# Placing matmul operands and split-weight buffers at fixed residues modulo 256 in a two-block float32 transformer kernel

## The chip, the cores and the metric

The kernel runs on one core of one Trainium2 chip, as one program launched once. The metric is the device time of an execution in microseconds (us). Five engines work side by side: TensorE (PE in the profile; its weight loads are shown apart as PEld), VectorE (DVE), ScalarE (ACT), GpSimd (POOL) and SyncE (SP), which here only issues DMAs.

## The reference, cut to what matters

Two model blocks follow each other on 256 tokens of width 2048, all in float32. The first has two layers (modulated norm, input projection to 8192 columns, gated convolution and two-way retention, output projection; layer 0 also carries 256 context tokens). The second has one layer (input projection, two attention branches, output projection, a gated feed-forward of width 5632, and a gated last projection). What takes the time are products with large weights:

```python
u = hx @ w_in                                     # first block, 2048 x 8192, two layers
x = x + gate[:, None] * (jnp.concatenate([y_conv, y_ret], axis=-1) @ w_out)
...
proj = h @ w_in[i]                                # second block, 2048 x 6144
x = x + rms_norm(o @ w_out[i], ln_mix_post[i])
g, u = jnp.split(h @ w_gate_up[i], 2, axis=-1)    # 2048 x 11264
f = (jax.nn.silu(g) * u) @ w_down[i]              # 5632 x 2048
gate = jax.nn.sigmoid(rms_norm(x, ln_pli[i]) @ w_pli_gate[i])
```

## The kernel before

**Split products.** Each weight tile (two slices of 128 rows by up to 512 columns) arrives by a DMA of SyncE's queue in a `raw` buffer (four of them). `split` then writes its rounded part `whi` on ScalarE (line 277) and the rest `wlo` on VectorE (line 278), each in one of three rotating buffers of 4096 bytes a partition. The activations are split in the same way (high part `xh`, low part `xl`, next to each other in one buffer). A product of weight and activation is the sum of hi by hi, hi by lo and lo by hi, all accumulated in PSUM; they are issued by `Block.steps` at line 332. A matmul has a stationary operand of 128 columns, which is loaded first (PEld), and a moving operand that streams past it. In the profile's rows the moving operand's tile is named behind PEld's: `mm<-a,whi` has moving `a` and stationary `whi`.

**Three forms of the product.** In mode "fm" the weights are stationary: with 512 tokens (layer 0, and k of layer 1) three products of 512 columns for each 128 by 128 weight; with 256 tokens ("wide") one product of 512 columns, whose moving operand is xh and xl one behind the other, and one of 256 columns (`wlo` with xh). In mode "tm" the activation is stationary and 512 columns of `whi` or `wlo` move. `a0` to `a15` hold the activations of the first block (high and low part 2048 bytes apart), `h0` to `h15`, `o0` to `o15` and `f0` to `f43` those of the second (1024 bytes apart).

**Order.** TensorE's order is that of the code (a manual schedule); what runs beside it (retention heads, attention heads, the modulation vectors of the next layer) is pumped in between the products. The other engines are ordered by the framework's scheduler. The start of the kernel (`mod0_cols`, lines 454 to 471) multiplies the conditioning vectors by `w_mod`, with a stationary operand of only 4 columns, woven with the first products of the layer.

**Where buffers lie.** The framework's pools place buffers one behind the other from low addresses; only the pool `ap` of `a0` to `a15` is filled from the top. An operand's address in its partition, modulo 256, follows from the sizes of all that lies below it. Buffers of 512 bytes or its multiples keep the residue from one 128-column slice to the next, so each group of products has one pair of residues throughout. The table in the section on the change has them.

**Decay masks.** `retention` builds four 128 by 128 masks for each head on ScalarE (lines 535 to 538) from the constant tile `cr`; `layer_tables` makes the decay rates `lg` and the vectors `dec` on VectorE (lines 516 and 522).

Of the kernel before, what the change touches and what calls it, by code (L numbers as in the profile page):

```python
# [14 lines left out]
ALU = mybir.AluOpType  # L15
# [12 lines left out]
PRI = 400  # L28
HOT = 1000
HS = 128.0 ** -0.5  # L30


CA = {}
# [4 lines left out]
def _layout(d, spec):  # L38
    o = 0
    for n, w in spec:  # L40
# [3 lines left out]


NCA = _layout(CA, [("ident", 128), ("ones", 128), ("comb", 2), ("nhalf", 8)])
NCR = _layout(CR, [("ropec", 256), ("ropes", 256), ("dabs", 128), ("dof", 128), ("dob", 128),
                   ("pos", 8)])
NCB = _layout(CB, [("negtri", 128), ("negones", 128), ("md", 128), ("cmul", 384),
                   ("onehot", 384), ("negm", 384)])  # L50

# [9 lines left out]
def constants():  # L61
    f = np.float32
    ca = np.zeros((P, NCA), f)
    ca[:, slice(*CA["ident"])] = np.eye(P, dtype=f)
    ca[:, slice(*CA["ones"])] = 1.0
    o = CA["comb"][0]
    ca[0, o] = ca[2, o] = ca[1, o + 1] = ca[3, o + 1] = 1.0
    ca[:, slice(*CA["nhalf"])] = -0.5

    cr = np.zeros((P, NCR), f)  # L70
    p = np.arange(P)
    t = np.arange(L)
    inv = f(10000.0) ** (-np.arange(32, dtype=f) / f(32))
    pos = np.where((p // 64)[:, None] == 0, (t // 64)[None], (t % 64)[None]).astype(f)
    ang = (pos * inv[p % 32][:, None]).astype(f)
    cr[:, slice(*CR["ropec"])] = np.cos(ang)
    sign = np.where(p % 64 < 32, -1.0, 1.0).astype(f)
    cr[:, slice(*CR["ropes"])] = np.sin(ang) * sign[:, None]
    j = p[:, None]
    i = p[None, :]  # L80
    cr[:, slice(*CR["dabs"])] = np.abs(i - j)
    cr[:, slice(*CR["dof"])] = 128 + i - j
    cr[:, slice(*CR["dob"])] = 128 + j - i
    o = CR["pos"][0]
    for a in range(2):
        tt = p + 128 * a
        cr[:, o + a] = tt + 1
        cr[:, o + 2 + a] = L - tt
        cr[:, o + 4 + a] = L - 1 - tt
        cr[:, o + 6 + a] = tt  # L90

    cb = np.zeros((P, NCB), f)
    cb[:, slice(*CB["negtri"])] = -(j > i).astype(f)
    cb[:, slice(*CB["negones"])] = -1.0
    cb[:, slice(*CB["md"])] = (j < i)
    d = 128 + p[:, None] - np.arange(256)[None]
    mult = (d >= 0) * ((d <= 128) * 1.0 + (d % 4 == 0) + (d % 16 == 0))
    o = CB["cmul"][0]
    cb[:, o:o + 256] = mult
    cb[:, o + 256:o + 384] = mult[:, 128:]  # L100
    x = np.arange(384)
    dd = 255 - x
    dc = np.maximum(dd, 1).astype(f)
    large = 16 + (np.log(dc / f(16)) / f(math.log(128.0)) * f(16)).astype(np.int32)
    large = np.minimum(large, 31)
    bucket = np.where(dd < 16, np.maximum(dd, 0), large)
    cb[:32, slice(*CB["onehot"])] = np.arange(32)[:, None] == bucket[None]
    bad = ~((dd >= 0) & ((dd <= 128) | (dd % 4 == 0)))
    cb[:, slice(*CB["negm"])] = np.where(bad, f(NEG), f(0))[None]
    return ca, cr, cb  # L110
# [3 lines left out]
def kernel(ctx: ExitStack, tc: tile.TileContext, x, c, cx, c_ctx, norm_w, w_mod, b_mod,  # L114
# [14 lines left out]

    consts = ctx.enter_context(tc.tile_pool(name="consts", bufs=1))  # L130
    wraw = ctx.enter_context(tc.tile_pool(name="wraw", bufs=4))
    wsp = ctx.enter_context(tc.tile_pool(name="wsp", bufs=3))
    rp = ctx.enter_context(tc.tile_pool(name="rp", bufs=1))
    sm = ctx.enter_context(tc.tile_pool(name="sm", bufs=2))
    tb = ctx.enter_context(tc.tile_pool(name="tb", bufs=3))
# [35 lines left out]
    vr_ = {}  # L171

    def load_vec(g):
        vr = mk(at, [P, 512], "sc")[:, :P] if g == 2 else mk(sm, [P, P], "vr", bufs=1)
        n0 = 0
        for n, cnt in VEC_ROWS[g]:
            nc.sync.dma_start(out=vr[n0:n0 + cnt, :], in_=srcs[n])
            V[n] = vecs[:, g * P + n0:g * P + n0 + cnt]
            n0 += cnt
        vr_[g] = vr, n0  # L180
# [87 lines left out]
    pri = [0]  # L268
    turn = [0]

    def split(raw, nk, width=512, parts=None):
        if parts is None:
            parts = (mk(wsp, [P, 2, 512], "whi", F32R)[:, :nk, :width],
                     mk(wsp, [P, 2, 512], "wlo", F32R)[:, :nk, :width])
        hi, lo = parts
        with tc.high_priority(offset=pri[0]):
            nc.scalar.copy(out=hi, in_=raw)  # L277
            nc.vector.tensor_tensor(out=lo, in0=raw, in1=hi, op=ALU.subtract)  # L278
        return hi, lo

    class Block:
# [17 lines left out]
        def load(self, kk, col, parts):  # L299
            c0, wd = col  # L300
            raw = mk(wraw, [P, 2, 512], "raw")[:, :len(kk), :wd]
            nc.sync.dma_start(out=raw, in_=self.w[kk[0] * P:(kk[0] + len(kk)) * P, c0:c0 + wd]
                              .rearrange("(k p) n -> p k n", p=P))
            return split(raw, len(kk), wd, parts)

        def steps(self, kk, parts=None):

# [46 lines left out]
    p1 = ExitStack()  # L354
    ap_ = p1.enter_context(tc.tile_pool(name="ap", bufs=1, side="right", reuse_waits="tile"))
    big = p1.enter_context(tc.tile_pool(name="big", bufs=1))
    t1 = p1.enter_context(tc.tile_pool(name="t1", bufs=1))
    st0 = ExitStack()
    wst = st0.enter_context(tc.tile_pool(name="wst", bufs=3))
# [17 lines left out]
    def R_(name):  # L377
        a, b = CR[name]
        return cr[:, a:b]
# [3 lines left out]
    load_x(0)  # L383
    load_x(1)
    turn_vec(0)
    s2 = mk(consts, [P, KT, 2], "s2")
    nc.scalar.activation(out=s2[:, :, 0], in_=V["c"], func=AF.Silu)
    nc.scalar.activation(out=s2[:, :, 1], in_=V["cctx"], func=AF.Silu)
    s4 = mk(t1, [P, KT, 4], "s4", F32R)
# [27 lines left out]
        rin[s] = rsq(mean_eps(ss[:, 0], 2, D), 2, f"rq{s}")  # L417


    modc = [[mk(consts, [P, 48], f"mod{l}{v}") for v in range(2)] for l in range(2)]  # L420

    def mod_bg(todo):

# [85 lines left out]
    def layer_tables(l):  # L509

        lg = []
        for d, src in enumerate((ret_decay_f, ret_decay_b)):
            e = mk(t1, [P, 8], f"lg{d}")
            nc.sync.dma_start(out=e, in_=src[l].partition_broadcast(P))
            nc.scalar.activation(out=e, in_=e, func=AF.Exp)
            nc.vector.tensor_scalar(out=e, in0=e, scalar1=-1.0, scalar2=None, op0=ALU.mult)
            lg.append(e)
        dec = mk(t1, [P, 4, 2, 8], "dec")
        o = CR["pos"][0]
        for q in range(4):  # L520
            for a in range(2):
                nc.vector.tensor_scalar(out=dec[:, q, a, :], in0=lg[q % 2],
                                        scalar1=cr[:, o + 2 * q + a:o + 2 * q + a + 1], scalar2=None,
                                        op0=ALU.mult)
        nc.scalar.activation(out=dec, in_=dec, func=AF.Exp)
        lgt["lg"], lgt["dec"] = lg, dec

    def retention(l, h, qT, kT, v, streams, Y):
# [5 lines left out]
        eb = dm[:, 3, :]  # L534
        nc.scalar.activation(out=dm[:, 0, :], in_=R_("dabs"), func=AF.Exp, scale=lgf)
        nc.scalar.activation(out=eb, in_=R_("dabs"), func=AF.Exp, scale=lgb)
        nc.scalar.activation(out=dm[:, 1, :], in_=R_("dof"), func=AF.Exp, scale=lgf)
        nc.scalar.activation(out=dm[:, 2, :], in_=R_("dob"), func=AF.Exp, scale=lgb)
        nc.gpsimd.affine_select(out=dm[:, 0, :], in_=dm[:, 0, :], pattern=[[1, P]], compare_op=ALU.is_ge,
                                fill=0.0, base=0, channel_multiplier=-1)  # L540
        nc.gpsimd.affine_select(out=eb, in_=eb, pattern=[[-1, P]], compare_op=ALU.is_ge,
# [400 lines left out]


    fl = mk(hp, [P, KT], "fl")
    nc.vector.tensor_tensor(out=fl, in0=V["fn"], in1=V["lpre"], op=ALU.mult)
    H = [hl(hp, f"h{k}") for k in range(KT)]
    with hot():
# [166 lines left out]
            vh["v"] = v  # L1114

    F = {}
    ss8 = mk(hp, [P, 2, 4], "ss8")
    part = mk(hp, [P, 2], "part")

    def project(w, mov, korder, split_at):  # L1120

# [169 lines left out]
```

## Time and profile before

| | |
|---|---|
| median of 3 runs | 2911.32 us (2911.03 to 2912.12) |
| the profiled execution | 2912.41 us |
| its span, first to last instruction | 2910.6 us |
| TensorE busy | 2875.3 us |
| VectorE, ScalarE, GpSimd busy | 1844.6, 1291.7, 81.6 us |
| mean granted TensorE clock | 0.997 of full speed |

The profiled execution took 1.8 us more than its span, and 1.1 us more than the median. TensorE's matmuls are pipelined: one starts while the one before still drains, so the time that a matmul costs is not its duration in a row but the distance from its start to the next start. A view in order of time shows the starts.

### The profile page before, as it was taken

How to read it: one execution, taken by the hardware profiler on the slowest of the kernel's cores; microseconds unless marked ns; L12 is line 12 of the kernel's file. 1: busy time of each engine (PE TensorE's matmuls, PEld its weight loads, DVE VectorE, ACT ScalarE, POOL GpSimd, SP SyncE). 2: the span in 40 equal slices, each digit the busy share in tenths (PEclk: the TensorE clock that was granted, in tenths of full speed). 3: DMA queues.
4: the chain of work that ended last, by engine and by line, in shares of the span. 5: the costliest groups of instructions: out<-in, count | busy, mean ns of one | idle time of the engine just before them, and what ended most of it. 6: DMA issues, size and time to landing. Idle time of an engine off the chain costs nothing.

```text
span 2910.6 us, 38166 instructions
## 1 busy us (share of the span) xinstructions
PE 2875.3 (99%) x14301; PEld 2376.3 (82%) x14301; DVE 1844.6 (63%) x3009; ACT 1291.7 (44%) x2048; POOL 81.6 (3%) x143
## 2 busy tenths in 40 slices
PE   7999999999999999999999999999999999999999
PEld 4678888888888878888888888887888888888878
DVE  7875765666677655664767766665755566544465
ACT  7643322242233233543545655554644444444354
POOL 0000000000000000000000010000000000000000
PEclk9999999999999999999999999999999999999999
DMA  9984445444556544654756665555566666655655
GB/s 306 294 250 141 127 152 159 146 136 141 159 170 192 164 140 144 211 174 149 227 174 218 199 196 167 167 167 181 161 187 188 185 186 187 188 187 189 201 169 166
DMA packets 299922, 527.09 MB, mean 181 GB/s; under 512 B 20016, under 2 KB 75800, under 8 KB 299480
## 3 DMA queue, kind: packets, MB, share of 16 engines
q1 hardware_dynamic: 296200, 513.23, 57.6%
q0 software_dynamic: 3392, 11.29, 1.3%
q8 instruction: 112, 1.84, 0.3%
q14 instruction: 74, 0.61, 0.1%
q10 hardware_dynamic: 144, 0.14, 0.0%
HBM read 509.88 MB, written 12.07 MB: 179 GB/s over the span
## 4 chain that ended last, share of the span: by engine, by line
PE 95%; DMA 2%; DVE 1%; ACT 1%; issue 0%; POOL 0%; SPq 0%; DVEq 0%; ACTq 0%; POOLq 0%
PE mm L332 88%; PE sd L466 2%; PE sd L581 1%; DMA raw<-in_w_mod_dram 1%; PE sd L568 1%; DVE wlo L278 1%; PE sd L332 0%; PE sd L575 0%; DMA raw<-in_w_in_dram 0%; PE sd L444 0%; PE sd L559 0%; ACT whi L277 0%; PE sd L479 0%; PE sd L1163 0%; DVE macc L438 0%
## 5 line engine op out<-in xcount | busy, mean ns | idle before, releaser
L278 DVE TENSOR_TENSOR wlo<-raw,whi 128x1024 fp32r<-128x1024 f32 (+1 forms) x812 | 977.4, 1207 | 822.5 <-ACT whi L277 801.5
L277 ACT CAST whi<-raw 128x1024 fp32r<-128x1024 f32 (+1 forms) x812 | 840.7, 1036 | 1392.1 <-PE mm L332 1165.8
L332 PE MATMUL mm<-a,whi 128*128 128x512 f32 x3392 | 1115.5, 398 | 1.5 <-ACT a L504 0.8
L332 PEld LDWEIGHTS mm<-a,whi 128*128 128x128 f32 x3392 | 634.9, 188 | 147.8 <-ACT a L504 1.2
L332 PE MATMUL mm<-a,wlo 128*128 128x512 f32 (+1 forms) x2208 | 755.4, 342 | 0.0
L332 PE MATMUL mm<-h,whi 128*128 128x512 f32 x1920 | 682.9, 397 | 0.1
L332 PE MATMUL mm<-h,wlo 128*128 128x256 f32 x1920 | 541.3, 282 | 0.0
L332 PEld LDWEIGHTS mm<-a,wlo 128*128 128x128 f32 x2208 | 415.4, 188 | 54.7
L332 PEld LDWEIGHTS mm<-h,whi 128*128 128x128 f32 x1920 | 360.9, 188 | 86.6 <-issue 0.6
L332 PEld LDWEIGHTS mm<-h,wlo 128*128 128x128 f32 x1920 | 360.8, 188 | 0.0
L438 DVE SCALAR_TENSOR_TENSOR macc<-raw,s,macc 128x512 f32<-128x512 f32 x420 | 291.8, 745 | 80.4 <-DMA raw<-in_w_mod_dram 79.1
L332 PE MATMUL mm<-whi,f 128*128 128x512 f32 x704 | 221.3, 395 | 0.0
L332 PE MATMUL mm<-whi,h 128*128 128x512 f32 (+1 forms) x576 | 173.4, 376 | 0.0
L332 PE MATMUL mm<-whi,a 128*128 128x512 f32 x512 | 161.8, 395 | 0.0
L332 PEld LDWEIGHTS mm<-whi,f 128*128 128x128 f32 x704 | 132.2, 188 | 32.0
L332 PE MATMUL mm<-wlo,f 128*128 128x512 f32 x352 | 139.0, 395 | 0.0
L332 PEld LDWEIGHTS mm<-whi,h 128*128 128x128 f32 x576 | 104.0, 188 | 18.7
L332 PEld LDWEIGHTS mm<-whi,a 128*128 128x128 f32 x512 | 96.1, 188 | 23.5
L332 PE MATMUL mm<-wlo,h 128*128 128x512 f32 (+1 forms) x288 | 106.5, 370 | 0.0
L332 PE MATMUL mm<-wlo,a 128*128 128x512 f32 x256 | 101.4, 396 | 0.0
L332 PE MATMUL mm<-whi,o 128*128 128x512 f32 x256 | 81.6, 396 | 0.0
L332 PEld LDWEIGHTS mm<-wlo,f 128*128 128x128 f32 x352 | 66.1, 188 | 16.1
(311 smaller groups left out, 2193.9 us busy)
## 6 DMA issues: line engine op xcount, KB each, us to landing
raw<-in_w_in_dram SPq DMA_DIRECT2D x344, 512.0 KB, 3.9
raw<-in_w_gate_up_dram SPq DMA_DIRECT2D x176, 512.0 KB, 3.7
raw<-in_w_mod_dram SPq DMA_DIRECT2D x128, 512.0 KB, 4.2
raw<-in_w_out_dram SPq DMA_DIRECT2D x96, 512.0 KB, 4.3
raw<-in_w_down_dram SPq DMA_DIRECT2D x88, 512.0 KB, 3.7
raw<-in_w_mod_dram SPq DMA_DIRECT2D x128, 256.0 KB, 5.6
raw<-in_w_pli_gate_dram SPq DMA_DIRECT2D x24, 512.0 KB, 4.6
raw<-in_w_in_dram SPq DMA_DIRECT2D x16, 256.0 KB, 5.0
```

Of the source, the lines that this page charges most:

```text
L277: nc.scalar.copy(out=hi, in_=raw)
L278: nc.vector.tensor_tensor(out=lo, in0=raw, in1=hi, op=ALU.subtract)
L332: nc.tensor.matmul(o[b], lhsT=l_, rhs=r_, start=d0 + a == 0 and b == 0, stop=d0 + a == self.nk - 1 and b == len(tri) - 1)
L438: nc.vector.scalar_tensor_tensor(out=acc[v], in0=raw[:, a, :], scalar=sc, in1=acc[v], op0=ALU.mult, op1=ALU.add)
L466: nc.tensor.matmul(pr[:4, :], lhsT=s4[:, kc + a, :], rhs=w[:, a, :], start=(kc + a == 0 and b == 0), stop=(kc + a == KT - 1 and b == 1))
L568: nc.tensor.matmul(ps[:, t * L:(t + 1) * L], lhsT=kT[:, q0 + t * P:q0 + (t + 1) * P], rhs=qT[:, q0:q0 + L], start=True, stop=True)
L581: nc.tensor.matmul(po[:, t * P:(t + 1) * P], lhsT=sc[:, jt * L + t * P:jt * L + (t + 1) * P], rhs=v[:, 2 * s + jt, :], start=(jt == 0), st ...
```

## The change

**Residues.** The split buffers become six buffers of 4128 bytes (`whi0` to `whi2`, `wlo0` to `wlo2`), each followed by a small buffer of 224 bytes, so that all six start at residue 192. Products that aren't wide use them from 32 bytes on, at residue 224; wide ones, and the products of `mod0_cols`, from the start. A pad in the pool `big`, and another in `hp`, together with `fl`, `ss8` and `part` allocated ahead of the activations, put `h`, `o`, `f`, `qT`, `kT`, `v` and `big0` at residue 224, where `a0` to `a15` already lay. The number of split buffers stays three of each; the index now runs in `ring`.

**Room.** The small vectors `s2` and `mod00` to `mod11` move into the gaps behind the split buffers. The rows of `load_vec` for groups 0 and 1 share the buffers `dg`. The constants `dof` and `dob` (128 + i - j and 128 + j - i) give way to one, `dsg` (i - j): the 128 times the rate is now the bias of the activation, out of a new small tile `lx` that takes three VectorE instructions a layer.

The residues (address in the partition modulo 256) that the built programs give the float32r products:

| products | count | moving: before, after | stationary: before, after |
|---|---|---|---|
| wide over `h`: `whi` 512 + `wlo` 256 columns | 1920 pairs | 128, 224 | 64, 192 |
| wide over `a`: `whi` 512 + `wlo` 256 columns | 1024 pairs | 224, 224 | 64, 192 |
| fm, 512 tokens, over `a` | 3552 | 224, 224 | 64, 224 |
| fm, 512 tokens, first weights in `v`, `qT`, `kT`, `big0` | 288 | 224, 224 | 128, 224 |
| tm, stationary `f` and `o` | 1440 | 64, 224 | 192, 224 |
| tm, stationary `a` | 768 | 64, 224 | 224, 224 |
| tm, stationary `h`, 512 columns | 672 | 64, 224 | 128, 224 |
| tm, stationary `h`, 256 columns | 192 | 64, 224 | 128, 224 |
| last input projection (`big0` stationary) | 48 | 64, 224 | 128, 224 |
| `mod0_cols`, 4 stationary columns | 256 | 64, 192 | every multiple of 16 in turn, the same |

```diff
-NCR = _layout(CR, [("ropec", 256), ("ropes", 256), ("dabs", 128), ("dof", 128), ("dob", 128),
-                   ("pos", 8)])
+NCR = _layout(CR, [("ropec", 256), ("ropes", 256), ("dabs", 128), ("dsg", 128), ("pos", 8)])
...
-    wsp = ctx.enter_context(tc.tile_pool(name="wsp", bufs=3))
+    wsp = ctx.enter_context(tc.tile_pool(name="wsp", bufs=1))
...
-        vr = mk(at, [P, 512], "sc")[:, :P] if g == 2 else mk(sm, [P, P], "vr", bufs=1)
+        vr = mk(at, [P, 512], "sc")[:, :P] if g == 2 else mk(sm, [P, P], "dg")
...
-    def split(raw, nk, width=512, parts=None):
+    WB = 3
+    ring = [0]
+    small = ["mod00", "mod01", "mod10", "mod11", "s2", "fill"]
+    smalls = {}
+    for i in range(WB):
+        for part in ("whi", "wlo"):
+            mk(wsp, [P, 1024 + STEP // 4], f"{part}{i}", F32R)
+            n = small.pop(0)
+            smalls[n] = mk(wsp, [P, (256 - STEP) // 4], n)
+
+    def shifted(tag, at):
+
+        b = mk(wsp, [P, 1024 + STEP // 4], tag, F32R)
+        return b[:, at // 4:at // 4 + 1024].rearrange("p (a n) -> p a n", a=2)
+
+    def split(raw, nk, width=512, parts=None, at=0):
         if parts is None:
-            parts = (mk(wsp, [P, 2, 512], "whi", F32R)[:, :nk, :width],
-                     mk(wsp, [P, 2, 512], "wlo", F32R)[:, :nk, :width])
+            ring[0] = (ring[0] + 1) % WB
+            parts = (shifted(f"whi{ring[0]}", at)[:, :nk, :width], shifted(f"wlo{ring[0]}", at)[:, :nk, :width])
...
-            return split(raw, len(kk), wd, parts)
+            return split(raw, len(kk), wd, parts, 0 if self.wide else STEP)
...
+    mk(big, [P, 56], "pad")
...
+        lx = mk(t1, [P, 3, 8], "lx")
+        for d in range(2):
+            nc.vector.tensor_scalar(out=lx[:, d, :], in0=lg[d], scalar1=float(P), scalar2=None, op0=ALU.mult)
+        nc.vector.tensor_scalar(out=lx[:, 2, :], in0=lg[1], scalar1=-1.0, scalar2=None, op0=ALU.mult)
+        lgt["lx"] = lx
...
-        nc.scalar.activation(out=dm[:, 1, :], in_=R_("dof"), func=AF.Exp, scale=lgf)
-        nc.scalar.activation(out=dm[:, 2, :], in_=R_("dob"), func=AF.Exp, scale=lgb)
+        lx = lgt["lx"]
+        nc.scalar.activation(out=dm[:, 1, :], in_=R_("dsg"), func=AF.Exp, scale=lgf, bias=lx[:, 0, h:h + 1])
+        nc.scalar.activation(out=dm[:, 2, :], in_=R_("dsg"), func=AF.Exp, scale=lx[:, 2, h:h + 1],
+                             bias=lx[:, 1, h:h + 1])
...
     fl = mk(hp, [P, KT], "fl")
+    ss8 = mk(hp, [P, 2, 4], "ss8")
+    part = mk(hp, [P, 2], "part")
+    mk(hp, [P, 40], "pad")
```

On TensorE a wide stretch over `h` in the feed-forward stands so before (numbers tell buffers apart; line 332):

```order
L332 MATMUL mm_18891<-h_3252_17512,whi_18963 128x512
L332 MATMUL mm_18891<-h_3252_17512,wlo_18964 128x256
L332 MATMUL mm_18892<-h_3250_17505,whi_18963 128x512
L332 MATMUL mm_18892<-h_3250_17505,wlo_18964 128x256
L332 MATMUL mm_18892<-h_3252_17512,whi_18963 128x512
L332 MATMUL mm_18892<-h_3252_17512,wlo_18964 128x256
```

and in the change (the same line is now 350):

```order
L350 MATMUL mm_18908<-h_3263_17529,whi_3545_18980 128x512
L350 MATMUL mm_18908<-h_3263_17529,wlo_3546_18981 128x256
L350 MATMUL mm_18909<-h_3261_17522,whi_3545_18980 128x512
L350 MATMUL mm_18909<-h_3261_17522,wlo_3546_18981 128x256
L350 MATMUL mm_18909<-h_3263_17529,whi_3545_18980 128x512
L350 MATMUL mm_18909<-h_3263_17529,wlo_3546_18981 128x256
```

Nothing moved: TensorE's 12200 rows stand in the same order in both programs, and only names and addresses differ.

On ScalarE, at the start of the first layer's retention, the masks of the first head (`dm_2273`) stand so before:

```order
L515 ACTIVATE lg_396_1699<-lg_396_1699 128x8
L535 ACTIVATE dm_2273<-cr_104,lg_395_1695 128x128
L537 ACTIVATE dm_2273<-cr_104,lg_395_1695 128x128
L536 ACTIVATE dm_2273<-cr_104,lg_396_1699 128x128
L538 ACTIVATE dm_2273<-cr_104,lg_396_1699 128x128
```

and so in the change (`dm_2285`):

```order
L534 ACTIVATE lg_404_1707<-lg_404_1707 128x8
L560 ACTIVATE dm_2285<-cr_117,lg_403_1703 128x128
L561 ACTIVATE dm_2285<-cr_117,lg_404_1707 128x128
L563 ACTIVATE dm_2285<-cr_117,lx_1711,lg_403_1703 128x128
L564 ACTIVATE dm_2285<-cr_117,lx_1711 128x128
```

The number of activations is the same; the two with the new constant now read `lx`, and stand behind the other two.

On VectorE, where the same layer's tables are made, the rows before are:

```order
L516 TENSOR_SCALAR lg_395_1695<-lg_395_1695 128x8
L522 TENSOR_SCALAR dec_1703<-lg_395_1695,cr_104 128x8 x4
L516 TENSOR_SCALAR lg_396_1699<-lg_396_1699 128x8
L522 TENSOR_SCALAR dec_1703<-lg_396_1699,cr_104 128x8 x3
L450 SCALAR_TENSOR_TENSOR mod_14_128<-sd_1575,vecs_87 128x2 x2
```

and in the change:

```order
L535 TENSOR_SCALAR lg_403_1703<-lg_403_1703 128x8
L540 TENSOR_SCALAR lx_1711<-lg_403_1703 128x8
L547 TENSOR_SCALAR dec_1715<-lg_403_1703,cr_117 128x8 x3
L535 TENSOR_SCALAR lg_404_1707<-lg_404_1707 128x8
L547 TENSOR_SCALAR dec_1715<-lg_403_1703,cr_117 128x8
L540 TENSOR_SCALAR lx_1711<-lg_404_1707 128x8
L541 TENSOR_SCALAR lx_1711<-lg_404_1707 128x8
```

Three instructions of 128x8 are new there, ahead of work that was next before.

## Rows read from the trace of the kernel before

**Rows 1.** The page: engines' busy time, and the chain that ended last.

```profile
PE 2875.3 (99%) x14301; PEld 2376.3 (82%) x14301; DVE 1844.6 (63%) x3009; ACT 1291.7 (44%) x2048; POOL 81.6 (3%) x143
...
PE 95%; DMA 2%; DVE 1%; ACT 1%; issue 0%; POOL 0%; SPq 0%; DVEq 0%; ACTq 0%; POOLq 0%
```

**Rows 2.** Stretches of the span: busy us and instructions of each engine, clock, DMA.

```profile
0.00:160.00 160.00, 140.50 (x633) 83.49 (x634) 125.87 (x225) 112.91 (x164) 2.76 (x10) 0.98 0.88 286
160.00:400.00 240.00, 240.00 (x1093) 195.94 (x1092) 161.21 (x296) 75.12 (x134) 12.54 (x24) 1.00 0.55 168
400.00:1650.00 1250.00, 1246.61 (x6031) 1036.51 (x6030) 808.29 (x1348) 476.60 (x776) 42.31 (x75) 1.00 0.55 170
1650.00:2911.00 1261.00, 1248.22 (x6549) 1060.32 (x6547) 749.26 (x1143) 627.11 (x977) 24.02 (x34) 1.00 0.60 181
```

**Rows 3.** TensorE's time in order, wide products over `h`: start us, duration us.

```profile
2399.64 0.40 PE L332 MATMUL mm<-h,whi 128*128 128x512 f32 x1
2399.87 0.28 PE L332 MATMUL mm<-h,wlo 128*128 128x256 f32 x1
...
2432.86 0.40 PE L332 MATMUL mm<-h,whi 128*128 128x512 f32 x1
```

**Rows 4.** The same view, wide products over `a` (second layer).

```profile
1173.81 0.28 PE L332 MATMUL mm<-a,wlo 128*128 128x256 f32 x1
1173.93 0.39 PE L332 MATMUL mm<-a,whi 128*128 128x512 f32 x1
...
1193.92 0.28 PE L332 MATMUL mm<-a,wlo 128*128 128x256 f32 x1
```

**Rows 5.** The same view, 512 tokens over `a`: three products each.

```profile
999.91 0.39 PE L332 MATMUL mm<-a,wlo 128*128 128x512 f32 x1
1000.14 0.64 PE L332 MATMUL mm<-a,whi 128*128 128x512 f32 x2
...
1028.73 0.40 PE L332 MATMUL mm<-a,wlo 128*128 128x512 f32 x1
```

**Rows 6.** The same view, tm with `f` stationary, then with `a`.

```profile
2559.89 0.39 PE L332 MATMUL mm<-wlo,f 128*128 128x512 f32 x1
2560.12 0.63 PE L332 MATMUL mm<-whi,f 128*128 128x512 f32 x2
...
2589.99 0.40 PE L332 MATMUL mm<-wlo,f 128*128 128x512 f32 x1
...
199.78 0.39 PE L332 MATMUL mm<-wlo,a 128*128 128x512 f32 x1
...
223.58 0.39 PE L332 MATMUL mm<-wlo,a 128*128 128x512 f32 x1
```

**Rows 7.** The same view, products with 4 stationary columns.

```profile
89.45 0.39 PE L466 MATMUL sd<-whi,s 128*4 128x512 f32 x1
...
91.07 0.40 PE L466 MATMUL sd<-wlo,s 128*4 128x512 f32 x1
```

**Rows 8.** Stretches of 10 us inside wide products over `h`, as in rows 2.

```profile
2350.00:2360.00 10.00, 10.00 (x58) 8.68 (x58) 8.80 (x16) 5.93 (x12) 0.00 (x0) 1.00 0.68 199
2360.00:2370.00 10.00, 10.00 (x59) 8.73 (x58) 3.71 (x4) 4.16 (x4) 0.00 (x0) 1.00 0.61 171
```

**Rows 9.** Small VectorE and ScalarE work: durations min, median, max in ns.

```profile
L516 DVE TENSOR_SCALAR lg<-lg x4: 159/160/171, 154.8 to 623.9; 128x8 f32<-128x8 f32 x4
L538 ACT ACTIVATE dm<-cr,lg x16: 384/388/416, 157.7 to 1424.2; 128x128 f32<-128x128 f32 x16
```

**Rows 10.** TensorE's longest waits: us in total, times, longest us.

```profile
PE sd L1163 <- DVE dg L1153: 6.4, 2, 3.9
PE sd L466 <- DVE wlo L278: 4.6, 7, 1.3
```

More of the change, by code (lines that the diff above doesn't have):

```diff
@@ L30 @@
 HS = 128.0 ** -0.5
+PLACE = 224
+STEP = 32
 CA = {}
@@ L81, in constants @@
     cr[:, slice(*CR["dabs"])] = np.abs(i - j)
-    cr[:, slice(*CR["dof"])] = 128 + i - j
-    cr[:, slice(*CR["dob"])] = 128 + j - i
+    cr[:, slice(*CR["dsg"])] = i - j
     o = CR["pos"][0]
@@ L385 @@
     turn_vec(0)
-    s2 = mk(consts, [P, KT, 2], "s2")
+    s2 = smalls["s2"][:, :2 * KT].rearrange("p (k v) -> p k v", v=2)
     nc.scalar.activation(out=s2[:, :, 0], in_=V["c"], func=AF.Silu)
@@ L417, in stream_in @@
         rin[s] = rsq(mean_eps(ss[:, 0], 2, D), 2, f"rq{s}")
-    modc = [[mk(consts, [P, 48], f"mod{l}{v}") for v in range(2)] for l in range(2)]
+    modc = [[smalls[f"mod{l}{v}"] for v in range(2)] for l in range(2)]
     def mod_bg(todo):
@@ L1116 @@
     F = {}
-    ss8 = mk(hp, [P, 2, 4], "ss8")
-    part = mk(hp, [P, 2], "part")
     def project(w, mov, korder, split_at):
```

## The prediction

> **What bounds the kernel now.** I read the page first. TensorE is busy for 2875.3 us, 99% of the span, and the chain that ended last runs 95% through it [rows 1]. The reader is to see that there is hardly a wait to remove: the time is what TensorE's products cost, one behind the other. The stretches say where that holds: in the first 160 us TensorE is idle for 19.5 us and the DMA engines are at 0.88; from there on it is idle for 16.2 us in all, and DMA is at 0.55 to 0.60 [rows 2]. Its longest waits behind the start are 6.4 us in total on `dg` and 4.6 us on `wlo` [rows 10]. A change that touches no product could thus bring or cost little.
>
> Then I read single products in order of time, from start to start. The granted clock is 1.00, the level of 2.4 GHz, so 512 columns at one a cycle would take 213.3 ns, and 768 would take 320.0 ns. The rows show more, and not the same everywhere:
>
> - wide over `h`: 94 pairs (512 and 256 columns) in 2432.86 - 2399.64 = 33.22 us, 353.4 ns a pair [rows 3];
> - wide over `a`, the same two shapes: 58 pairs in 20.11 us, 346.7 ns a pair [rows 4];
> - 512 tokens over `a`: 41 triples in 28.82 us, 234.3 ns a product [rows 5];
> - tm: 43 triples in 30.10 us with `f` stationary and 34 triples in 23.80 us with `a`, 233.3 ns a product for both [rows 6];
> - products with 4 stationary columns: 7 steps in 1.62 us, 231.4 ns [rows 7].
>
> All lie 8 to 10% above one column a cycle. Per 512 columns the two wide forms are 353.4 x 2/3 = 235.6 and 346.7 x 2/3 = 231.1 ns. So identical work differs by 1.9% between two places, and what differs between them is the address: moving operand at residue 128 in `h`, at 224 in `a`, stationary at 64 in both (and the distance of the two halves of the moving operand). The difference of a pair, 6.7 ns, is 16 columns.
>
> Is it contention with other engines? In two stretches of 10 us over `h`, VectorE is busy for 8.80 and 3.71 us and ScalarE for 5.93 and 4.16 us, and TensorE starts 58 and 59 products [rows 8]. It isn't.
>
> The Trainium skill speaks against the change here: "TensorE: Matmul & The Clock Gate" says under "Step-by-step: what each phase is for" that moving operand and weight load have read ports of their own, so that loading the next weights takes nothing from the running matmul. By that no address could matter, and the sum below would be zero. The trace disagrees so far: 353.4 against 346.7 ns for the same shapes.
>
> **The change part by part.**
>
> *Wide over `h`, 1920 pairs.* The moving operand goes from 128 to 224, where `a` lies; the stationary one from 64 to 192. The nearest row is the pair over `a` with the same moving residue [rows 4]. Value taken: 346.7 ns, so 1920 x 6.7 ns = 12.9 us less. Bounds: no change (if it is the halves' distance that differs), and the same 6.7 ns more.
>
> *Wide over `a`, 1024 pairs.* Only the stationary residue moves, 64 to 192. It is already at the lowest step that the rows show; taken as unchanged, with 1024 x 6.7 = 6.9 us as the bound of a loss, and nothing known below.
>
> *512-column products.* 3552 over `a` at 234.3 ns [rows 5], and 288 + 1440 + 768 + 672 + 48 = 3216 taken at 233.3 ns, by the two groups of rows 6. All 6768 end with both operands at residue 224, a pair that no row shows. What the rows show is that three pairs of residues apart by 96 or 128 give 233.3 ns (`f` and `o` have 64 and 192, `a` has 64 and 224), that a distance of 160 gives 234.3, and that 231.1 to 231.4 is the lowest [rows 4, 7]. The lower bound is 231.1, the upper one the 235.6 of the wide form over `h`. I take the middle of the two levels next to the present one, 232.2 ns: (231.1 + 233.3)/2. That gives 3552 x 2.1 = 7.5 us and 3216 x 1.1 = 3.5 us, 11.0 us less; at 233.3 it would be 3.6 us, at 231.1 18.4 us (3552 x 3.2 + 3216 x 2.2).
>
> *The 192 products of 256 columns and the 256 with 4 stationary columns.* At one step of a few ns either way under 1 us; taken at nothing.
>
> *Masks and tables.* TensorE's order is the same row by row. ScalarE has as many masks as before, at a median of 388 ns; VectorE has six instructions of 128x8 more in all, near the 160 ns of line 516, 1.0 us [rows 9]. VectorE and ScalarE are busy for 67% and 31% of the stretch from 160 to 400 us, where the first lie, while TensorE is never idle there [rows 2]; the work of TensorE hides them. Bare they would cost that 1.0 us. The constant tile is 512 bytes a row shorter: nothing. `vr` shares `dg` only before and between its uses in `bcast_rows`; the wait on `dg` of 6.4 us comes from line 1153, long after the last `vr` [rows 10], and stays. The rotation of the split buffers still has three of each, so VectorE and ScalarE get ahead of TensorE as far as before.
>
> *Sum.* 12.9 + 11.0 = 23.9 us less. From the profiled execution's 2912.4 us (2910.6 of span and 1.8 around it) that gives 2888.5; it lay 1.1 us above the median of the runs, so for the median 2911.3 - 23.9 = 2887.4, say 2887 us. Little of it lies in the first 160 us, where loads could take it back.
>
> **The rivals.**
>
> *Deeper.* With both operands at one residue the 512-column products lose one more unit of 16 columns, from 233.3 to 226.7 ns. Then 3552 x 7.6 + 3216 x 6.6 = 48.2 us, and with `h` 61 us less: 2850 us. For it: the spread of a pair is one such unit, so units come off. Against it: with nearly nothing to load for the stationary operand the step is still 231.4 ns [rows 7], so no row goes below that.
>
> *No change.* Shape decides, not address: the 512-column moving operand over `h` is one run, the one over `a` two runs 2048 bytes apart, and that alone makes the 6.7 ns. Then nothing moves: 2911 us. For it: three pairs of residues agree at 233.3 ns. It is also what the skill's rule on separate ports comes to. Against it: a run broken in two should not be the cheaper one.
>
> *Slower: lockstep.* A 512-column product now starts its moving stream at the residue at which the next weights' load starts. If the two hinder each other from the first read on, and each product pays one unit of 16 columns more than the 233.3, it takes 240.0 ns: 3552 x 5.7 + 3216 x 6.7 = 41.8 us more, less the 12.9 of `h`: 2940 us. It decides from 12.9 us / 6768 = 1.9 ns a product on, a step of about 235.7 ns. For it: residues 64 apart give the highest level shown, those farther apart lower ones. Against it: the order isn't strict, since 160 gives both 234.3 and 231.1.
>
> **How the numbers follow.** Forecast case (wide over `h` joins `a`, 512-column products end between 231.1 and 233.3 ns): 0.60, a range of its own of 2880 to 2895. Only the 512-column products gain, `h` stays: 0.05, 2893 to 2908. Deeper: 0.10, around 2850. No change: 0.12, 2908 to 2914. Lockstep, whole or in part: 0.13, 2917 to 2940. What a measurement of this kernel can tell from no change is about 0.2%, 5.8 us. Faster by more than that: 0.60 + 0.05 + 0.10 = 0.75; within it 0.12; slower 0.13. The range reaches from 2866, below the forecast case and into the first part of the deeper one, to 2914, with no change inside; it leaves out most of the deeper case and lockstep, about 0.2.
>
> **What would show it.** In the changed kernel's view in order of time: pairs over `h` at 346.7 ns instead of 353.4; triples over `a` and tm triples at 693 to 700 ns; pairs over `a` still at 346.7. TensorE's idle time should stay near 35 us, and its instructions' counts the same. The prediction is wrong if the pairs over `h` stay at 353 (no change), if any group of 512-column products goes above 235.7 (lockstep) or below 230 (deeper), or if TensorE's waits grow by more than some microseconds, which would mean that the buffers, not the addresses, made the difference.

## The result, and the profile after

The changed kernel takes 2860.2 us (median of 4 runs, 2858.7 to 2860.62), against 2911.18 us for the kernel before on the same chip (4 runs, 2909.8 to 2912.12): a ratio of 0.9824, with a 95% interval of 0.9807 to 0.9841. The forecast was 2887 us with a range of 2866 to 2914. The sign was right, the size was not: the gain is 51 us, not 24, and the time lies 6 us below the range, near the rival "deeper".

The page after, engines' busy time:

```profile
PE 2822.7 (99%) x14301; PEld 2374.8 (83%) x14301; DVE 1840.7 (64%) x3015; ACT 1293.8 (45%) x2048; POOL 81.3 (3%) x143
```

The count of TensorE's instructions is that of [rows 1], and its busy time fell by 52.6 us, which is the whole of the gain (the span fell from 2910.6 to 2858.4 us). The first three stretches after, in the columns of [rows 2]:

```profile
0.00:160.00 160.00, 141.48 (x632) 84.30 (x633) 125.33 (x227) 112.58 (x163) 2.76 (x10) 0.97 0.88 287
160.00:400.00 240.00, 239.29 (x1110) 198.47 (x1109) 164.66 (x304) 78.29 (x138) 12.54 (x24) 1.00 0.55 167
400.00:1650.00 1250.00, 1246.22 (x6175) 1057.44 (x6174) 826.60 (x1392) 493.00 (x800) 44.33 (x77) 1.00 0.57 175
```

In the first 160 us as many products run as before (632, before 633): nothing was gained there. From then on the same stretch holds more products (1110 instead of 1093, 6175 instead of 6031) at the same clock and the same lack of idle time. So the products themselves became shorter, and the rows in order of time say which. Wide over `a`, as [rows 4], then wide over `h`, as [rows 3]:

```profile
1149.82 0.39 PE L350 MATMUL mm<-a,whi 128*128 128x512 f32 x1
...
1169.92 0.39 PE L350 MATMUL mm<-a,whi 128*128 128x512 f32 x1
...
2369.90 0.39 PE L350 MATMUL mm<-h,whi 128*128 128x512 f32 x1
...
2399.71 0.39 PE L350 MATMUL mm<-h,whi 128*128 128x512 f32 x1
```

Over `a` 58 pairs take 20.10 us, 346.6 ns a pair, as before. Over `h` 86 pairs take 29.81 us, 346.6 ns instead of 353.4. Then 512 tokens over `a`, as [rows 5], and tm with `f` stationary, as [rows 6]:

```profile
389.73 0.39 PE L350 MATMUL mm<-a,wlo 128*128 128x512 f32 x1
...
415.57 0.39 PE L350 MATMUL mm<-a,wlo 128*128 128x512 f32 x1
...
2514.62 0.39 PE L350 MATMUL mm<-wlo,f 128*128 128x512 f32 x1
...
2548.62 0.39 PE L350 MATMUL mm<-wlo,f 128*128 128x512 f32 x1
```

38 triples in 25.84 us and 50 triples in 34.00 us are 680.0 ns a triple in both: 226.7 ns a product, instead of 234.3 and 233.3. That is 5.5 ns below the value taken in the forecast, and 4.4 below its lower bound of 231.1. The 192 products of 256 columns went the other way:

```profile
2830.44 0.28 PE L350 MATMUL mm<-wlo,h 128*128 128x256 f32 x1
...
2842.68 0.28 PE L350 MATMUL mm<-wlo,h 128*128 128x256 f32 x1
```

34 triples in 12.24 us, 120.0 ns a product, against 117.8 by the steps of the trace before: 0.4 us in all. The waits of [rows 10] stand as they were:

```profile
PE sd L1191 <- DVE dg L1181: 6.4, 2, 3.9
PE sd L485 <- DVE wlo L296: 4.8, 6, 2.1
```

TensorE's order is the same in both programs, so each product's step (from its start to the next start) can be set against its own step before. Summed over groups the difference is, in us:

| group | change |
|---|---|
| fm, 512 tokens, over `a` | -25.0, and +1.3 where the next instruction is side work |
| wide over `h` | -12.1 |
| tm, 512 columns: `f`, `a`, `h`, `o` | -7.0, -4.2, -2.4, -2.2 |
| tm, 256 columns | +0.4 |
| `mod0_cols` | +1.5 |
| lines 1163 and 479 | -1.3, -1.1 |
| all | -52.3 |

### The profile page after: what moved, and what is told of

It reads as the page before. It is cut to its first block, busy times and chain, and to the rows that moved or that the text cites. A ratio compares the mean times of both kernels' runs of the same rounds, so it can differ in the third digit from the quotient of the medians.

```text
span 2858.4 us, 38172 instructions
## 1 busy us (share of the span) xinstructions
PE 2822.7 (99%) x14301; PEld 2374.8 (83%) x14301; DVE 1840.7 (64%) x3015; ACT 1293.8 (45%) x2048; POOL 81.3 (3%) x143
## 4 chain that ended last, share of the span: by engine, by line
PE 94%; DVE 2%; DMA 2%; issue 1%; ACT 0%; SPq 0%; POOL 0%; DVEq 0%; ACTq 0%; POOLq 0%
PE mm L350 87%; PE sd L485 2%; DMA raw<-in_w_mod_dram 1%; PE sd L608 1%; PE sd L595 1%; DVE wlo L296 1%; DVE macc L457 1%; PE sd L602 0%; PE sd L586 0%; PE sd L350 0%; PE sd L463 0%; ACT whi L295 0%; PE sd L498 0%; POOL rq L195 0%; PE sd L635 0%
## 5 line engine op out<-in xcount | busy, mean ns | idle before, releaser
L350 PE MATMUL mm<-a,whi 128*128 128x512 f32 x3392 | 1099.1, 393 | 0.3 <-ACT a L523 0.3
L350 PE MATMUL mm<-h,whi 128*128 128x512 f32 x1920 | 670.8, 392 | 0.5 <-DVE h L965 0.5
```

What stands on the lines that cost most here:

```text
L350: nc.tensor.matmul(o[b], lhsT=l_, rhs=r_, start=d0 + a == 0 and b == 0, stop=d0 + a == self.nk - 1 and b == len(tri) - 1)
```

## The experiments

The question was what decides a product's step. Theory D: only the distance between moving and stationary address, modulo 256. Rival R: the residue 224 is itself a good place for the moving operand. Rival E: what changed is how other engines' traffic meets TensorE's. In all programs of products alone, the moving and the stationary operands are eight buffers each, at every multiple of 32; names end in `a` (residue 0) to `h` (residue 224).

**Products alone (`m1_residues`).** Each run is 60 products of one pair of buffers, one behind the other, for 512 columns, wide pairs, 256 columns, and narrow stationary operands; all of the reference's work is left out. The part for 512 columns, where `let` is "abcdefgh" and `plain` issues the 60 products, reads:

```python
for m in "had":
    for s in let:
        plain(m, s)
```

> Products alone, no other work: 60 matmuls in a row for each pair of residues of moving and stationary operand (multiples of 32), moving at 224, 0 and 96 with 512 columns, and for the wide and the 256-column form with moving at 224 and 0. Theory D (only the distance of the two residues modulo 256 decides): the eight steps with moving at 0 and at 96 are those with moving at 224, shifted; distance 0 gives 226.7 ns for 512 columns and 120 ns for 256, distance 32 gives 346.7 ns for a wide pair, and some other distances give 233 to 236. Rival R (the moving residue of 224 by itself is what helps): 226.7 ns with moving at 224 whatever the stationary residue, and 233 or more with moving at 0 and 96. Rival E (the other engines' accesses make the step): all near one level here. With 4, 32 and 64 stationary columns: if the units of 16 columns are paid to the weight load, the step falls toward 213 to 216 ns as the load shrinks.

One execution took 785.55 us. In order of time, with moving residue 224, then 0, then 96, and at last 4 and 64 stationary columns (each row but the last shows only the first nine products of a run of 60, the last one a whole run; the step is the distance between the starts of two neighbouring runs, divided by 60):

```profile
37.89 2.27 PE L70 MATMUL acc<-mh,sa 128*128 128x512 f32 x9
51.89 2.26 PE L70 MATMUL acc<-mh,sb 128*128 128x512 f32 x9
65.89 2.27 PE L70 MATMUL acc<-mh,sc 128*128 128x512 f32 x9
79.94 2.25 PE L70 MATMUL acc<-mh,sd 128*128 128x512 f32 x9
93.88 2.26 PE L70 MATMUL acc<-mh,se 128*128 128x512 f32 x9
107.88 2.23 PE L70 MATMUL acc<-mh,sf 128*128 128x512 f32 x9
121.62 2.26 PE L70 MATMUL acc<-mh,sg 128*128 128x512 f32 x9
135.62 2.20 PE L70 MATMUL acc<-mh,sh 128*128 128x512 f32 x9
149.22 2.23 PE L70 MATMUL acc<-ma,sa 128*128 128x512 f32 x9
162.86 2.26 PE L70 MATMUL acc<-ma,sb 128*128 128x512 f32 x9
...
302.31 2.20 PE L70 MATMUL acc<-md,sd 128*128 128x512 f32 x9
315.92 2.26 PE L70 MATMUL acc<-md,se 128*128 128x512 f32 x9
...
653.70 2.24 PE L70 MATMUL acc<-mh,sh 128*4 128x512 f32 x9
667.56 2.24 PE L70 MATMUL acc<-mh,sc 128*4 128x512 f32 x9
...
722.96 13.76 PE L70 MATMUL acc<-mh,sc 128*64 128x512 f32 x60
```

With the moving operand at 224 the steps for stationary residues 0, 32, ... 224 are 233.3, 233.3, 234.2, 232.3, 233.3, 229.0, 233.3 and, for both at 224, (149.22 - 135.62)/60 = 226.7 ns. With the moving operand at 0 it is the stationary one at 0 that gives 227.3 (162.86 - 149.22), with 96 the one at 96, 226.8 (315.92 - 302.31). By distance (moving minus stationary) the three series of 512 columns agree within 0.7 ns, and the two series of wide pairs as well (the mean of pairs 11 to 29 of each run of 30):

| distance | 0 | 32 | 64 | 96 | 128 | 160 | 192 | 224 |
|---|---|---|---|---|---|---|---|---|
| 512 columns, ns | 226.7 | 233.3 | 228.9 | 233.3 | 232.2 | 234.2 | 233.3 | 233.3 |
| wide pair, ns | 353.4 | 346.7 | 348.8 | 349.9 | 351.2 | 346.7 | 353.3 | 353.7 |

For 512 columns this is theory D. R falls (224 is no better than 0 or 96), and E too: nothing else runs here. For 256 columns D holds only in part: six of the eight distances agree between moving at 224 and at 0 within 0.3 ns, but 192 gives 113.4 and 117.9 ns, and 160 gives 120.0 and 117.3. The table also gives what the traces show: for wide pairs 160 is the 346.7 of `a` before, and 32 that of all after; for 512 columns 160 is the 234.3 of before, 96 its 233.3, and 0 the 226.7 of after. Two of before fit less well: tm over `f` and `o` (distance 128) had 233.3 in the kernel and 232.2 here, wide over `h` (64) 353.4 and 348.8 (`m2_mixed_residues` below has 353.1 at that same distance). And the row with 4 stationary columns is at 231.0 ns at distance 0 and at 160 alike, above the 226.6 of 64 columns at 160 (the last row: 13.76 us, less a last product of 0.39, over 59 steps) and the 226.7 of 128 columns at 0. So the 231.4 of [rows 7] was no floor.

**The shift undone (`e2_all_at_192`).** In the changed kernel, the non-wide products take their weights from the start of the buffer:

```diff
-            return split(raw, len(kk), wd, parts, 0 if self.wide else STEP)
+            return split(raw, len(kk), wd, parts, 0)
```

> The change, with the 32 bytes undone: all products take weights at residue 192. Theory D: wide products stay at 346.7 ns a pair; products of 512 columns over a are then at distance 32 and tm products at distance 224, both unknown distances, and lose what the change gave them: 231 to 236 ns instead of 226.7, 29 to 63 us more, 2889 to 2923 us. Rival R: products over a (moving at 224) stay at 226.7, only tm products (moving at 192) may lose, at most 22 us: 2860 to 2882 us.

Measured: 2897.35 us (2895.85 to 2898.5), ratio to the kernel before 0.9952 (0.9936 to 0.9969). 512 tokens over `a` (distance 32), then wide over `h`:

```profile
389.82 0.40 PE L350 MATMUL mm<-a,wlo 128*128 128x512 f32 x1
...
415.72 0.39 PE L350 MATMUL mm<-a,wlo 128*128 128x512 f32 x1
...
2399.82 0.39 PE L350 MATMUL mm<-h,whi 128*128 128x512 f32 x1
...
2429.98 0.39 PE L350 MATMUL mm<-h,whi 128*128 128x512 f32 x1
```

37 triples in 25.90 us, 233.3 ns a product; 87 wide pairs in 30.16 us, 346.7 ns a pair. So the 32 bytes alone are worth 37 us, and what is left is the part of `h`.

**Activations alone (`e4_activations_only`).** In the kernel before, one pad moves `h` from 128 to 224 and `o` and `f` from 192 to 32; the split buffers stay at 64:

```diff
     fl = mk(hp, [P, KT], "fl")
+    mk(hp, [P, 24], "pad")
```

> The kernel before with one pad of 96 bytes ahead of h: h goes from residue 128 to 224, o and f from 192 to 32, the split buffers stay at 64. Theory D: wide pairs over h get the distance of 160 that pairs over a have, 346.7 instead of 353.4 ns, 12.9 us less; tm products over f and o go from distance 128 to 32, unknown, 226.7 to 236 ns: 2889 to 2902 us. If the distance of the two halves of the moving operand, not its residue, made wide over h dearer: 2911 us.

Measured: 2900.65 us (2900.05 to 2902.3), ratio 0.9966 (0.9953 to 0.9979). Wide over `h` (now at distance 160, as `a` before), then tm over `f` (distance 32 instead of 128):

```profile
2399.89 0.39 PE L332 MATMUL mm<-h,whi 128*128 128x512 f32 x1
...
2429.70 0.39 PE L332 MATMUL mm<-h,whi 128*128 128x512 f32 x1
...
2560.09 0.40 PE L332 MATMUL mm<-wlo,f 128*128 128x512 f32 x1
...
2584.59 0.39 PE L332 MATMUL mm<-wlo,f 128*128 128x512 f32 x1
```

86 pairs in 29.81 us are 346.6 ns; 35 triples in 24.50 us are 700.0, 233.3 a product. One pad of 96 bytes thus brings 10.6 us against the 2911.27 us of before on that chip, nearly all of the wide term.

**Wide ones at 224 too (`e3_all_at_224`).** The same line of the changed kernel, with `STEP` for all products:

> The change, with wide products too taking weights 32 bytes in, at 224: distance 0 for all. Theory D: the products of 512 columns stay at 226.7 ns; a wide pair goes from 346.7 to 346.7 (226.7 + 120.0, if each product keeps its own cost at distance 0) or up to 360 ns: 2860 to 2899 us. Rival R: no change, 2860 us.

Measured: 2863.18 us (2861.89 to 2864.32), ratio 0.9837 (0.9822 to 0.9851). At distance 0 the wide pairs over `a` run at two levels, in one and the same group of residues; early and late ones:

```profile
1148.93 0.40 PE L350 MATMUL mm<-a,whi 128*128 128x512 f32 x1
...
1164.83 0.40 PE L350 MATMUL mm<-a,whi 128*128 128x512 f32 x1
...
1462.97 0.39 PE L350 MATMUL mm<-a,whi 128*128 128x512 f32 x1
...
1479.96 0.39 PE L350 MATMUL mm<-a,whi 128*128 128x512 f32 x1
```

45 pairs in 15.90 us are 353.3 ns, 49 pairs in 16.99 us are 346.7. Within each of the two stretches the level stays what it is; the 512-column products stay at 226.7. Over `h`, at the same distance, most pairs run at 346.7. Over all wide pairs the steps add up to 2.9 us more than in the changed kernel, where distance 32 gives them the lower level: about the 3 us between the two medians, though the intervals of the two ratios overlap.

**Masks and tables alone (`e5_masks_only`).** The kernel before with `dsg`, `lx` and `vr` in `dg`, and no address of a product changed:

```diff
-        nc.scalar.activation(out=dm[:, 1, :], in_=R_("dof"), func=AF.Exp, scale=lgf)
-        nc.scalar.activation(out=dm[:, 2, :], in_=R_("dob"), func=AF.Exp, scale=lgb)
+        nc.scalar.activation(out=dm[:, 1, :], in_=R_("dsg"), func=AF.Exp, scale=lgf, bias=lx[:, 0, h:h + 1])
+        nc.scalar.activation(out=dm[:, 2, :], in_=R_("dsg"), func=AF.Exp, scale=lx[:, 2, h:h + 1],
+                             bias=lx[:, 1, h:h + 1])
```

> The kernel before with the part of the change that only makes room: one mask constant instead of two, the small tile lx, vr in the buffers of dg; all addresses of the products as before. If the work that was costed at nothing is hidden: 2911 us, within 0.2%. If it carries some of the 51 us that the change gave: below 2905 us.

Measured: 2912.96 us (10 runs, 2910.88 to 2914.73) against 2912.65 (13 runs); ratio 1.0 (0.9991 to 1.001). Taken at nothing, it is nothing.

**Finer distances and mixed pairs (`m2_mixed_residues`).** Products alone again: wide pairs whose two stationary operands lie at residues chosen apart (64 combinations), then 512 columns with the stationary operand moved in steps of 8 bytes.

> Products alone again. (1) Wide pairs with moving at 224 and the stationary operand of the 512-column product and that of the 256-column product at residues of their own, all 64 pairs of multiples of 32. A theory in which a product's cost follows from the distance between its moving operand and the stationary operand that is loaded meanwhile, that of the next product, lets the two be chosen apart: 226.7 ns (distance 0, for the one loaded during the 512 columns) plus 113.3 ns (distance 192, the lowest 256-column step seen) would be 340.0 ns a pair against the 346.7 of the change. The rival: the two products' phases tie them together, and no pair goes below 346.7 ns. (2) 512 columns with the stationary operand at every multiple of 8 bytes: distance 0 is the only one at 226.7 ns, or a finer place lies below it. (3) 64 stationary columns at the eight residues: with half the load the best distance moves away from 0.

The 64 pairs took 346.3 to 353.7 ns: the lowest is within 0.4 ns of the 346.7 that the changed kernel has, so its wide form can't be had cheaper this way. Two of the 64 have both stationary operands at one residue and repeat a pair of `m1_residues`, yet at another level: both at 224 (distance 0), then, from earlier in the run, both at 160 (distance 64):

```profile
700.62 0.39 PE L69 MATMUL acc<-mh,sh 128*128 128x512 f32 x1
...
710.67 0.39 PE L69 MATMUL acc<-mh,sh 128*128 128x512 f32 x1
...
512.14 0.40 PE L69 MATMUL acc<-mh,sf 128*128 128x512 f32 x1
...
522.38 0.40 PE L69 MATMUL acc<-mh,sf 128*128 128x512 f32 x1
```

29 pairs take 10.05 us, 346.6 ns a pair, where `m1_residues` had 353.4; and 10.24 us, 353.1 ns, where it had 348.8. With 64 stationary columns distance 160 takes 231.5 ns here and took 226.6 there. So for wide pairs and for narrow loads the distance alone doesn't fix the step, even with nothing else running. For 512 columns the multiples of 32 come out as in `m1_residues` within 0.5 ns. In steps of 8 bytes only distances 0 and 136 give 226.7 ns; 8 gives 233.3, 16 228.3, 24 231.1, 248 230.7, 240 233.4. Neighbours 8 bytes apart differ by a whole unit (6.7 ns). Windows of 10 us in order of time, at distance 0, 248 and 8, each merged to one row:

```profile
713.78 10.59 PE L76 MATMUL acc<-mh,sh 128*128 128x512 f32 x46
...
725.82 10.54 PE L76 MATMUL acc<-mh,sh 128*128 128x512 f32 x45
...
1143.82 10.43 PE L76 MATMUL acc<-mh,sh 128*128 128x512 f32 x44
```

Less the last product's own 0.39 us these are 10.20 / 45 = 226.7, 10.15 / 44 = 230.7 and 10.04 / 43 = 233.5 ns from start to start, for the same two buffers. In the run at distance 0 the first steps are 230, 233, 236, 224, 231, 236, 228, 233, 231 ns, and only then 226.7: the level is approached here, not met at once. (The run of `m1_residues` with both operands at 224 was at 226.7 from its first step.)

**Grouped wide products (`m3_grouped`).** Products alone, with 2, 4 or 8 products of each of the two wide shapes behind one another, to see whether the 512-column ones then reach 226.7:

> Products alone: the wide pair's two products in groups, 2, 4 or 8 of 512 columns and then as many of 256, moving at 224, the stationary operand of the 512 columns at 224, 192, 0 or 32 and that of the 256 columns at each multiple of 32. If a run of one shape keeps that shape's own step (226.7 ns at distance 0, 113.3 to 120 ns), a pair falls from 346.7 to 340.0 to 346.7 ns, lowest for the longest groups with stationary residues 224 and 32. If the two shapes stay tied by a common phase, as in the run before, no arrangement goes below 346.7 ns.

The lowest step of all arrangements is 346.4 ns a pair, the highest 360. Groups of eight with the stationary operands at 224 and 32, where 340.0 was expected if each shape kept its own step, take about 347 ns a pair. Grouping brings nothing.

**Eight bytes off (`e6_eight_bytes_off`).** Back in the whole kernel, the finest test of theory D: the changed kernel with a shift of 24 bytes instead of 32.

```diff
-            return split(raw, len(kk), wd, parts, 0 if self.wide else STEP)
+            return split(raw, len(kk), wd, parts, 0 if self.wide else 24)
```

> The changed kernel with the shift of the 512-column products' weights at 24 bytes instead of 32, so that their stationary operand lies 8 bytes nearer its buffer's start: distance 8 from the moving operand in the products that build the first block, 248 in the transposed ones. Nothing else is changed. If the exact distance decides, as the products alone had it (233.3 ns at 8, 230.7 at 248, against 226.7 at 0), the 3552 products at 8 give back 6.6 ns each, 23.5 us, and the 2928 at 248 4.0 ns each, 11.8 us: about 2895 us, and the trace shows 233.3 and 230.7. If an address counts only by its slot of 32 bytes or more, or if the gain of the 512-column products came from elsewhere in the change, nothing moves: 2860 us and 226.7 in both.

Measured: 2895.3 us (2894.09 to 2895.6), ratio 0.9942 (0.9927 to 0.9957). 512 tokens over `a` (distance 8), then tm over `f` (248):

```profile
389.94 0.39 PE L350 MATMUL mm<-a,wlo 128*128 128x512 f32 x1
...
415.84 0.40 PE L350 MATMUL mm<-a,wlo 128*128 128x512 f32 x1
...
2544.86 0.39 PE L350 MATMUL mm<-wlo,f 128*128 128x512 f32 x1
...
2574.81 0.39 PE L350 MATMUL mm<-wlo,f 128*128 128x512 f32 x1
```

37 triples in 25.90 us, 233.3 ns a product, as the products alone had it; 43 triples in 29.95 us, 232.2 a product, 1.5 more than there. Eight bytes of 256 give back 35 of the 51 us. The time met the expected 2895 us, though partly by two errors that cancel: 3552 x 6.6 + 2928 x 5.5 ns are 39.5 us, and 35.1 were measured. The tm products at 248 don't follow the products alone to the nanosecond.

**Short blocks apart (`e7_short_blocks_apart`).** The changed kernel, with the buffers of 256-wide blocks 64 bytes apart from the rest, at residue 160:

```diff
+            if width == 256:
+                parts = tuple(p[:, :, 48:304] for p in (shifted(f"whi{ring[0]}", STEP), shifted(f"wlo{ring[0]}", STEP)))
```

> The changed kernel with the split weights' buffers of the blocks that are 256 wide at residue 160 instead of 192. It puts the 192 transposed products of 256 columns at distance 192, where the products alone took 113.3 to 117.8 ns against 120.0 at 0, and as a side effect 96 first-block products of 512 columns at distance 64, 228.9 instead of 226.7 ns. Distance theory: 192 times 2.2 to 6.7 ns less, 0.4 to 1.3 us, and 96 times 2.2 more, 0.2 us: 0.2 to 1.1 us less, about 2859.5 us, which only the steps in the trace can show. If the 256-column step of the change (120.0) has another cause than the distance, it stays at 120.0 and the time at 2860 us.

Measured: 2858.72 us (2858.19 to 2859.06), ratio 0.9817 (0.98 to 0.9833); the changed kernel itself had 0.9824 (0.9807 to 0.9841) in another comparison, so the two can't be told apart by time. The 256-column products:

```profile
2829.68 0.28 PE L352 MATMUL mm<-wlo,h 128*128 128x256 f32 x1
...
2832.86 0.28 PE L352 MATMUL mm<-wlo,h 128*128 128x256 f32 x1
```

9 triples in 3.18 us are 353.3 ns, 117.8 a product, where the changed kernel has 120.0 (above). The 0.4 us that the change lost there is a matter of distance as well.

## Why the prediction was wrong

**Right: the address decides, not the shape and not other engines.** The step was read from [rows 3, 4] in the prediction and is borne out by `m1_residues` and, in the kernel, by `e6_eight_bytes_off`. The rivals "no change" and "lockstep" fall: no group of 512-column products rose, though both operands now start at one residue. The Trainium skill ("TensorE: Matmul & The Clock Gate", "Step-by-step: what each phase is for") gives moving operand and weight load read ports of their own, from which the prediction drew that no address could matter; the measurements differ: 226.7 to 234.2 ns for the same product, by the distance of the two addresses.

**Right in the number, with luck in the reason: wide over `h`.** Taken at 12.9 us; 12.1 by the matched rows, and 10.6 us by `e4_activations_only` alone. The forecast took the step of `a` because the moving residue becomes that of `a`, 224. That residue doesn't decide: with the moving operand at 224, `m1_residues` has 346.7 to 353.7 ns by the stationary one. The distance went from 64 to 32, that of `a` before was 160, and it is by luck that 32 and 160 share the lowest level. The same luck kept wide over `a` where it was, when its distance went from 160 to 32. Wide over `a` stayed at 346.7 ns, masks and tables cost nothing, and the waits stayed.

**Wrong: the 512-column term.** The failing step is the value taken for the pair of residues that no row showed: "I take the middle of the two levels next to the present one, 232.2 ns", with 231.1 as the lower bound. Measured: 226.7. The term of 11.0 us came to 39.5 (25.0 + 7.0 + 4.2 + 2.4 + 2.2 - 1.3). Behind it stood the argument against the rival "deeper", that with nearly nothing to load the step is still 231.4 ns [rows 7], "so no row goes below that". It took the narrow load for a floor. `m1_residues` shows that it is none: 4 stationary columns take 231.0 ns, 64 take 226.6 to 232.7 (with `m2_mixed_residues`) and 128 take 226.7 to 234.2; a smaller load is not a cheaper one. What was shown was only that no row *of that kernel* went below, and none with 128 stationary columns had the distance 0.

**"Deeper" was the mechanism, and 9 us short of its price.** By its steps (7.6 and 6.6 ns a product, with `h`) it came to 61 us; 52.3 were measured in the rows. Where the rest went:

- The 288 products with the first weights, most of them in the first 160 us, gained less than 0.3 us of 288 x 6.6 = 1.9, so some 1.6 us are missing there. TensorE is idle there for 18.5 us (19.5 in [rows 2]) at a DMA share of 0.88, and as many products run as before. That loads give the pace there was seen in the prediction, and not counted.
- Behind side work the products don't run at their level at once. The rows of one such place, after:

```profile
384.27 1.04 PE L463 MATMUL sd<-ca,macc 128*128 128x128 f32 x8
...
385.62 0.40 PE L350 MATMUL mm<-a,wlo 128*128 128x512 f32 x1
...
387.69 0.39 PE L350 MATMUL mm<-a,wlo 128*128 128x512 f32 x1
...
388.37 0.39 PE L350 MATMUL mm<-a,wlo 128*128 128x512 f32 x1
```

The row at 384.27 is side work (line 463). From 385.62 to 387.69 three triples take 2.07 us, 230.0 ns a product; the next takes 0.68 us, the steady 226.7. The kernel has 225 such places, 59 of them ahead of 512 tokens over `a` and 48 ahead of tm. Summed over the first twelve products behind each, what lies above the steady step is 5.9 us before and 8.7 after for 512 tokens over `a`, and 3.9 and 6.2 us for tm: 5.1 us that the change didn't get. The last products ahead of side work stand 2.27 instead of 0.56 us, and 7.62 instead of 7.41, above that step: 1.9 us. Other engines don't make the approach: from 385.38 on the steps are 233, 236, 224, 231, 236, 228, 233, 231 ns and then 226.7, to the nanosecond those of the products alone at distance 0 (`m2_mixed_residues`). What the chip does in these products stays open.

1.6 + 5.1 + 1.9 = 8.6 us, about all that is missing. `e6_eight_bytes_off` fits: there the steps say 39.5 us, the time 35, and the first twelve products behind side work lose only 3.6 of the 7.5 us that the steady steps give for them.

## What to carry to other kernels

When TensorE never waits, look at the start-to-start distance of its products, group by group: equal shapes at unequal steps mean that something as cheap as an address is worth moving (here 1.8% of the kernel for pads and a 32-byte shift, and 35 us of it lost again by 8 bytes). A lowest value among the rows at hand is the lowest of the settings that happen to be there, not a floor; where a setting is new, a few runs of products alone, over all distances, give the price before any kernel is rearranged (here for 512 columns within 1.5 ns of the kernel's own step). What steady steps times counts promise has to be cut by the stretches that loads pace and by the products that follow interruptions (here 9 of 61 us).

## What the runs showed of the hardware that was not expected

- The steady step of a 512-column float32r product with a new stationary operand of 128 columns each time depends on the distance of the two addresses modulo 256, and on 8 bytes of it: 226.7 ns at 0 and 136, 228.3 to 234.2 elsewhere. Frequent levels are whole units of 6.67 ns, 16 columns at 2.4 GHz: 226.7 is 544 columns' time, 233.3 is 560, 346.7 for a wide pair is 832, 353.3 is 848. What in the chip makes the units, and why 0 and 136 are short of one, stays open; the runs show no order by size of distance.
- The cheapest distance isn't one for all shapes: 0 is the best for 512 columns with 128 stationary columns, but with 64 it takes 230.0 ns, where distance 64 takes 228.4 (`m2_mixed_residues`), and for 256 columns 119.8, among the dearest.
- One distance can have two stable levels (wide pairs at distance 0 in `e3_all_at_224`, 346.7 and 353.3 ns). It isn't a matter of the other engines: alone, distance 0 took 353.4 ns in `m1_residues` and 346.6 in `m2_mixed_residues`, and distance 64 took 348.8 and 353.1. What selects the level was not settled.
- Behind an interruption the level is mostly approached over up to some ten products, with one and the same row of steps in the kernel and alone (233, 236, 224, 231, 236, 228, 233, 231, then 226.7 ns, or an end part of it).
- The Trainium skill ("TensorE: Matmul & The Clock Gate", "Wait — 56ns, not 53.3ns?") has 215.7 ns from start to start for 512 columns at the higher clock. No steady step of these float32r runs, all with a weight load for each product, came below 226.6 ns.
